# A two-layer backbone kernel: all of v by seven half-size products, partial weight sums by accumulating transfers, the condition stream moved into the heads

## The chip, the cores and the metric

One core of one Trainium2 chip. The metric is device time in microseconds of one execution. Times of before: median 1779.65 us of 3 runs, 1779.38 to 1782.42.

## What is computed

Two layers over 512 latent tokens of width 2048 (and 256 context tokens in the first). The first layer is an even one (mLSTM heads, pooling groups, one output projection), the second an odd one, where the change lies. Of the reference:

```python
sh_l, sc_l, g_l = ada_params(c, ada_w[layer], ada_b[layer])   # silu(c) @ w + b
xm_l = x_lat * (1.0 + sc_l) + sh_l
...
def sgu_mixer(xm, w_in, ln_g, ln_b, w_sp, b_sp):
    u, v, z = jnp.split(xm @ w_in, 3, axis=-1)       # each 2048 wide
    v = layer_norm(v, ln_g, ln_b)
    s = jnp.einsum('hts,bnshc->bnthc', w_sp, vh) + b_sp.T[None, None, :, :, None]
    return u * s.reshape(bsz, seqlen, D_SGU) * jax.nn.silu(z)
...
x_lat = layer_norm(DEEPNORM_ALPHA * x_lat + g_l * (y_l @ w_out_odd[j]), post_ln_g[layer], post_ln_b[layer])
```

## The kernel before, in words

Every float32 operand of a matmul is split in two float32r parts, a rounded one (`hi`, a cast on ScalarE) and the rest (`lo`, a difference on VectorE): `split`, L104 to L106. A product a x b is then three products on TensorE: hi x hi, hi x lo, lo x hi. The program is written in one order; `Flow` (L36) is a planner that counts TensorE time, and lets side tasks (generators that yield how many us to wait) put in their instructions between the products when they are due; `drain` forces the rest of a task out.

**Weights.** The loads of all weights are issued on the SP queue, in program order, 512 KB each. In `ahead` (L159 to L174) a load goes to one of three `wraw` buffers and its two halves are split into `whl` buffers. `newest` holds the newest split's VectorE instruction; a side task that issues under `tc.issue_after(newest[0].ins)` puts its instruction behind that one on VectorE's queue.

**The condition stream.** `ada` (L268 to L292) computes silu(c) @ ada_w on VectorE: 128 steps, each a load of 512 KB into one of three `araw` buffers (SP queue) and one 128x1024 product with an accumulated sum, L280. Its first 96 steps (`ada(range(12), ...)`, L822) are spawned at the first head, one per 2.8 us of planned time. The last 32 steps (`range(12, 16)`, the gate of the second layer) are spawned after the first column block of the first output projection, one per 5.6 us.

**The first output projection.** `out_phase` (L937) with `out0`: column blocks 0 to 2 for all four token blocks, then block 3 for the first 256 tokens, then for the last 256. When a half of the tokens is complete it is normalised, and `finish0` (L1032) transposes it on TensorE, modulates it on ScalarE (L1051, into `mr`) and splits it into `m` (L1052); the first half while the second is multiplied.

**The second layer's input projection.** v (2048 columns): the first 1024 columns are two column blocks by `form_b` (L195), full products of 16 blocks, in the order (0, first half), (0, second half), (1, all), `vseq`; meanwhile `combine` forms the sums of x's quarters (a22 - a21, a11 - (a22 - a21) and so on). The other 1024 columns of v, then z and u in halves, are five jobs of `quarters` (L1131): each takes the 512x2048 by 2048x1024 product as a 2x2 block product with seven half-size products (Winograd's form), numbered 1 to 7. Products 1, 2 and 4 take quarters of x as they are, 3, 5, 6 and 7 take sums. The sums of the weights' quarters are made on VectorE: `t1` = piece 0 + piece 1 (L1169), piece 1 + piece 3 (L1174), `t1` + piece 3 (L1179), piece 2 + `t1` (L1184). A job has 28 steps (7 products x 4 blocks of depth), each of 12 products on TensorE and one split of a 128x1024 unit. Units lie in 7 buffers (4 `whl`, 3 `araw`), raw loads in 4 (3 `wraw`, 1 `crw0`); the split runs `QAHEAD` = 2 steps ahead of the products in program order.

After that come the spatial mixing (`spatial`, a side task on v, which takes the reciprocal deviations from GpSimd, L249), z and u gates, and the second output projection, which is not touched.

Of the kernel before, what the change touches and what calls it, by code (L numbers as in the profile page):

```python
# [16 lines left out]
P = 128  # L17
# [51 lines left out]
def tile_backbone(ctx: ExitStack, tc: tile.TileContext, io: dict, out: bass.AP):  # L69
# [65 lines left out]
    vseq = [(0, H0), (0, H1), (1, ALL)]  # L135
# [3 lines left out]
    for c, _ in vseq:  # L139
        stream += b_raws(io["wv"], c)  # L140
# [3 lines left out]
    raws, parts, used, newest = [], [], [0], [None]  # L144
# [14 lines left out]
    def ahead(p):  # L159
        while len(parts) < min(p + AHEAD + 1, 2 * upto[0]):  # L160
# [107 lines left out]
    def ada(cs, pace):  # L268
        steps = [(f, k) for c in cs for f in range(4 * c, 4 * c + 4) for k in range(2)]
        ts, part = [], None  # L270
        for n, (f, k) in enumerate(steps):
# [6 lines left out]
            if n % 8 == 0:  # L278
                part = cst.tile([P, 4, 2], F32, tag="part", name=nm("part"), bufs=2)
            ve.scalar_tensor_tensor(ts[n], ts[n], 0.5, crow[k], ALU.mult, ALU.mult,  # L280
                                    accum_out=part[:, f % 4, k:k + 1])
# [13 lines left out]
    with ExitStack() as ev:  # L295
# [641 lines left out]
    def out_phase(seq, resid, gate, order, before, norm, finish, hold=0, affine=(), second=None):  # L937
# [15 lines left out]
        def product(c, tbs, before, hold):  # L953
# [3 lines left out]
            def ready(n):  # L957
                if before is not None:
                    before(n)
                if n == KB // 2:  # L960
# [27 lines left out]
        for n, (c, tbs) in enumerate(seq):  # L988
            if n == 1 and second is not None:
                second()  # L990
            for pts in product(c, tbs, before if n == 0 else None, hold if n == len(seq) - 1 else 0):
# [40 lines left out]
    def finish0(hf, z):  # L1032
# [3 lines left out]
        yield 4.0  # L1036
        for k2 in range(8):
# [10 lines left out]
            for j in range(2):  # L1048
                kb = 2 * k2 + j
                m[hf][kb] = big.tile([P, 2, NC], F32R, tag=f"{tag}{kb}", name=nm("xn"))  # L1050
                sc.activation(xt[:, j], pt[:, j * NC:(j + 1) * NC], AF.Identity, bias=B[:, kb:kb + 1], scale=G[:, kb:kb + 1])  # L1051
                split(xt[:, j], m[hf][kb][:, 0, :], m[hf][kb][:, 1, :])  # L1052
# [4 lines left out]
    t_ada2 = []  # L1057
    t_n = out_phase(out0, io["x"], gd[0:1], yorder, y0_ready, norm0, finish0,
                    second=lambda: t_ada2.append(fl.spawn(ada(range(12, 16), lambda n: 5.6))))


    def m_stat(kb, t):
        s = slice((t % 2) * P, (t % 2 + 1) * P)
        return m[t // 2][kb][:, 0, s], m[t // 2][kb][:, 1, s]
# [3 lines left out]

    def v_evac(pts, c):
        for t, pt in pts.items():  # L1070
            s = slice(c * 512, (c + 1) * 512)
            if v[t] is None:
                v[t] = la.tile([P, D], F32, tag=f"z{t}", name=nm("v"))
            sc.copy(v[t][:, s], pt)
            ve.bn_stats(vst[t][:, c, :], v[t][:, s])
# [10 lines left out]
    def combine():  # L1086


        for g in range(4):
            a11, a12, a21, a22 = (mr[i][g + 4 * j] for i in range(2) for j in range(2))  # L1090
            for o, x_, y_, op in ((a22, a22, a21, ALU.subtract), (a21, a11, a21, ALU.subtract),
                                  (a11, a11, a22, ALU.add), (a12, a11, a12, ALU.subtract)):
                with tc.issue_after(newest[0].ins):
                    ve.tensor_tensor(o, x_, y_, op)
                yield PACE
            comb[5, g], comb[7, g], comb[6, g], comb[3, g] = a22, a21, a11, a12
        free = [f"xl{n}" for n in (8, 9, 10, 11, 12, 13, 14, 15, 3, 4, 5, 6, 7, 0, 1, 2)]
        for n in range(8):
            with tc.issue_after(newest[0].ins):
                comb_split((5, 7)[n // 4], n % 4, *((big, tag) for tag in free[2 * n:2 * n + 2]))  # L1100
            yield PACE

    PACE = 2.2
# [5 lines left out]

    def combine2():  # L1110
        for g in range(4):
            comb_split(3, g, (big, f"xh{2 * g}"), (big, f"xh{2 * g + 1}"))
            yield 3.0
        free = [f"mr{n}" for n in (4, 5, 6, 7, 0, 1, 2)] + ["mx"]
        for g in range(4):
            comb_split(6, g, (la, free[2 * g]), (la, free[2 * g + 1]))
            yield 3.0
# [10 lines left out]
    QAHEAD = 2  # L1128
    BUFS = {"wraw": 3, "araw": 3, "whl": 4, "crw0": 1}

    def quarters(jobs):  # L1131


        steps = []
        for n in range(len(jobs)):
            for group in ((1, 5, 7), (2, 3), (6,), (4,)):
                steps += [(n, p_, j) for j in range(4) for p_ in group]
        need = {1: (1, 0), 5: (), 7: (3,), 2: (2,), 3: (3,), 6: (), 4: (2,)}
        loads = [(jobs[n][0], j, piece) for n, p_, j in steps for piece in need[p_]]
        rtags, utags = ["wraw"] * 3 + ["crw0"], ["whl"] * 4 + ["araw"] * 3  # L1140
        n_u = [0]
        raw, made = [], []
        taken = [0]

        def load_to(k):
            while len(raw) < min(k, len(loads)):
                tag = rtags[len(raw) % len(rtags)]
                r = wp.tile([P, 1024], F32, tag=tag, name=nm("qr"), bufs=BUFS[tag])
                q, j, piece = loads[len(raw)]
                dma.dma_start(r, io["wq"][q, j, piece])  # L1150
                raw.append(r)

        def take():
            taken[0] += 1
            load_to(taken[0] + len(rtags) - 1)
            return raw[taken[0] - 1]

        def unit():
            tag = utags[n_u[0] % len(utags)]
            n_u[0] += 1  # L1160
            return wp.tile([P, 1024], F32R, tag=tag, name=nm("wh"), bufs=BUFS[tag])

        t1, b12 = {}, {}

        def prep(n, p_, j):
            if p_ == 1:
                b12[j], x_ = take(), take()
                t1[j] = pair_tile(j)
                ve.tensor_tensor(t1[j], x_, b12[j], ALU.add)  # L1169
            elif p_ == 5:  # L1170
                x_ = t1[j]
            elif p_ == 7:
                x_ = b12[j]
                ve.tensor_tensor(x_, x_, take(), ALU.add)  # L1174
            elif p_ == 2:
                x_ = take()
            elif p_ == 3:
                x_ = take()
                ve.tensor_tensor(t1[j], t1[j], x_, ALU.add)  # L1179
            elif p_ == 6:  # L1180
                x_ = t1[j]
            else:
                x_ = take()
                ve.tensor_tensor(x_, x_, t1[j], ALU.add)  # L1184
            made.append((unit(), unit()))
            newest[0] = split(x_, *made[-1])

        bank = {}
        for i, (n, p_, j) in enumerate(steps):
            while len(made) < min(i + 1 + QAHEAD, len(steps)):  # L1190
                prep(*steps[len(made)])
            at_ = {1: 1, 2: 1, 5: 5, 3: 5, 7: 7, 4: 7, 6: 6}[p_]
            if j == 0 and p_ in (1, 5, 7, 6):
                bank[p_] = [ps() for _ in range(2)]
            pts = bank[at_]
# [309 lines left out]
```

## Time and profile before

| what | value |
|---|---|
| median of 3 runs | 1779.65 us |
| the profiled execution | 1778.18 us |
| its span | 1776.4 us |
| mean granted clock of TensorE | 0.995 |
| TensorE busy | 1735.3 us, 98% of the span |
| VectorE, ScalarE, GpSimd busy | 1215.0, 691.1, 35.0 us |
| moved by DMA | 343.58 MB, mean 193 GB/s |

The span runs from the first to the last instruction of the core; the time of the execution contains it. Busy shares are means over stages with different limits, so each stage is read by itself: the first layer's heads end and its output projection begins at about 894 us, the v stage at 1081, the seven-product stage at 1178, the second output projection at 1588. Windows give busy time and count of records per engine in a stretch, then the granted clock (1.00 is 2.4 GHz) and what the DMA engines did. Matmuls are pipelined: the step from one start to the next is the cost of one, not its duration.

### The profile page before, as it was taken

The numbers are of one execution on the slowest core, as the hardware profiler recorded it, in microseconds if no ns is written. First come the engines' busy times: TensorE is split into PE (matmuls) and PEld (weight loads), VectorE is DVE, ScalarE is ACT, GpSimd is POOL, SyncE is SP. The second block draws the span as 40 slices with busy tenths as digits, with TensorE's granted clock in tenths as the row PEclk, the third lists the DMA queues.
The fourth block names the chain that finished last, engine by engine and source line by source line (L and its number), as shares of the span: only waits on it lengthen the run. The fifth ranks groups of instructions, "written<-read, shape, count | busy, mean of one in ns | idle before, by whom it ended". The sixth has DMA issues, their size and how long they took to land.

```text
span 1776.4 us, 23519 instructions
## 1 busy us (share of the span) xinstructions
PE 1735.3 (98%) x8656; PEld 1419.5 (80%) x8656; DVE 1215.0 (68%) x2140; ACT 691.1 (39%) x1239; POOL 35.0 (2%) x65
## 2 busy tenths in 40 slices
PE   8999999999999999999999999999999999999996
PEld 5677788888788888888887787788888888888884
DVE  4545597778775554564658676767988878875557
ACT  3222332224454355345332247534454444532220
POOL 0000000000000000000000000000000000000004
PEclk9999999999999999999999999999999999999998
DMA  9986298899542332432289656544555454555443
GB/s 370 354 309 232 89 335 312 314 324 358 191 157 84 125 119 87 139 105 73 100 285 327 221 189 215 162 138 158 171 164 180 148 191 137 175 159 167 134 131 106
DMA packets 131130, 343.58 MB, mean 193 GB/s; under 512 B 12622, under 2 KB 22822, under 8 KB 130502
## 3 DMA queue, kind: packets, MB, share of 16 engines
q1 hardware_dynamic: 128710, 335.78, 55.8%
q10 hardware_dynamic: 2304, 6.29, 0.9%
q8 instruction: 68, 1.11, 0.3%
q14 instruction: 48, 0.39, 0.1%
HBM read 319.96 MB, written 22.07 MB: 193 GB/s over the span
## 4 chain that ended last, share of the span: by engine, by line
PE 74%; DMA 13%; DVE 9%; ACT 2%; issue 2%; POOL 0%; SPq 0%; POOLq 0%; DVEq 0%; ACTq 0%
DMA adw<-in_adat_dram 10%; PE ps L1204 7%; PE ps L1203 7%; PE ps L1205 7%; PE ps L187 6%; PE ps L192 6%; PE ps L188 6%; PE ps L204 5%; PE ps L203 5%; PE ps L205 5%; DVE adw L280 3%; PE ps L408 2%; PE ps L410 2%; PE ps L409 2%; PE ps L640 2%
## 5 line engine op out<-in xcount | busy, mean ns | idle before, releaser
L105 ACT CAST wh<-wr 128x512 fp32r<-128x512 f32 x400 | 246.4, 623 | 475.8 <-PE ps L205 173.1
L106 DVE TENSOR_TENSOR wh<-wr,wh 128x512 fp32r<-128x512 f32 x392 | 266.8, 686 | 198.3 <-ACT wh L105 197.0
L187 PE MATMUL ps<-xh,wh 128*128 128x512 f32 x704 | 278.0, 395 | 0.0
L192 PE MATMUL ps<-xh,wh 128*128 128x512 f32 x704 | 275.2, 391 | 0.4 <-DVE wh L106 0.4
L188 PE MATMUL ps<-xl,wh 128*128 128x512 f32 x704 | 275.3, 391 | 0.0
L205 PE MATMUL ps<-wh,yl 128*128 128x512 f32 x512 | 200.2, 391 | 0.0
L204 PE MATMUL ps<-wh,yh 128*128 128x512 f32 x480 | 188.7, 393 | 4.8 <-DVE wh L106 4.8
L203 PE MATMUL ps<-wh,yh 128*128 128x512 f32 x512 | 193.1, 392 | 0.2 <-ACT wh L105 0.2
L280 DVE SCALAR_TENSOR_TENSOR adw<-adw,crow 128x1024 f32<-128x1024 f32 x128 | 156.0, 1220 | 53.7 <-DMA adw<-in_adat_dram 53.0
L192 PEld LDWEIGHTS ps<-xh,wh 128*128 128x128 f32 x704 | 132.2, 188 | 29.2 <-DVE wh L106 0.8
L105 ACT CAST wh<-qr 128x1024 fp32r<-128x1024 f32 x100 | 104.6, 1052 | 128.3 <-PE ps L1205 50.5
L187 PEld LDWEIGHTS ps<-xh,wh 128*128 128x128 f32 x704 | 132.5, 188 | 21.8 <-issue 0.7
L188 PEld LDWEIGHTS ps<-xl,wh 128*128 128x128 f32 x704 | 132.6, 188 | 21.6 <-issue 0.7
L106 DVE TENSOR_TENSOR wh<-qr,wh 128x1024 fp32r<-128x1024 f32 x100 | 121.3, 1218 | 11.5 <-issue 6.4
L1204 PE MATMUL ps<-wh,ch 128*128 128x512 f32 x320 | 126.8, 396 | 0.0
L1205 PE MATMUL ps<-wh,ch 128*128 128x512 f32 x320 | 125.0, 391 | 0.0
L1203 PE MATMUL ps<-wh,ch 128*128 128x512 f32 x320 | 117.6, 396 | 0.0
L203 PEld LDWEIGHTS ps<-wh,yh 128*128 128x128 f32 x512 | 96.4, 189 | 20.9 <-ACT wh L105 1.0
L205 PEld LDWEIGHTS ps<-wh,yl 128*128 128x128 f32 x512 | 96.6, 189 | 19.7
L204 PEld LDWEIGHTS ps<-wh,yh 128*128 128x128 f32 x480 | 90.5, 189 | 26.3 <-DVE wh L106 7.8
L1204 PE MATMUL ps<-wh,xn 128*128 128x512 f32 x240 | 93.7, 390 | 0.0
L1205 PE MATMUL ps<-wh,xn 128*128 128x512 f32 x240 | 93.5, 390 | 0.0
(303 smaller groups left out, 2956.6 us busy)
## 6 DMA issues: line engine op xcount, KB each, us to landing
adw<-in_adat_dram SPq DMA_DIRECT2D x128, 512.0 KB, 5.8
qr<-in_wq_dram SPq DMA_DIRECT2D x120, 512.0 KB, 3.4
wr<-in_wie_dram SPq DMA_DIRECT2D x96, 512.0 KB, 3.6
aw<-in_a_dram SPq DMA_DIRECT2D x64, 512.0 KB, 7.0
wr<-in_woe_dram SPq DMA_DIRECT2D x40, 512.0 KB, 4.9
wr<-in_woo_dram SPq DMA_DIRECT2D x32, 512.0 KB, 3.8
wr<-in_wv_dram SPq DMA_DIRECT2D x24, 512.0 KB, 4.2
w<-in_wie_dram SPq DMA_DIRECT2D x28, 256.0 KB, 4.9
```

The costliest lines, as they stand in the source:

```text
L105: sc.copy(hi, src)
L106: return ve.tensor_tensor(lo, src, f32(hi), ALU.subtract)
L187: te.matmul(pt[:, :n], a, xh_, start=first, stop=False)
L188: te.matmul(pt[:, :n], a, xl_, start=False, stop=False)
L192: te.matmul(pt[:, :n], b, xh_, start=False, stop=last)
L203: te.matmul(pts[t], a, wh, start=n == 0, stop=False)
L204: te.matmul(pts[t], a, wl, start=False, stop=False)
L205: te.matmul(pts[t], b, wh, start=False, stop=n == KB - 1)
L280: ve.scalar_tensor_tensor(ts[n], ts[n], 0.5, crow[k], ALU.mult, ALU.mult, accum_out=part[:, f % 4, k:k + 1])
L1203: te.matmul(pts[t], a, wh[:, s], start=first, stop=False, **more)
L1204: te.matmul(pts[t], a, wl[:, s], start=False, stop=False, **more)
L1205: te.matmul(pts[t], b, wh[:, s], start=False, stop=end, **more)
```

## The change

All of v goes by seven half-size products, as two jobs at the head of the list, six jobs in all. For these two (`first` = 2), products 1 and 2, which need the first 256 tokens only, come first for both jobs, 16 steps; then, per job, 5 and 7 alternating, then 3, 6 and 4. The first unit's split and the first four loads are issued at block 12 of 16 of the projection's last product (`late`). `finish0` of the second half starts 14 us of planned time later than at first 4, in another order, and leaves out the split of the quarter that no product takes as it is. `combine` and `combine2` become one task with a pace of 1.7 us.

A part of the weights' sums is made by transfers that GpSimd issues with `accum_op=ALU.add`, from HBM onto a tile in SBUF. In the two v jobs these are all four sums of a depth block (for product 5: load piece 1 into `t1`, add piece 0; for 7: load piece 1, add piece 3; after product 5's split add piece 3 to `t1`; after product 6's split add piece 2). In the other four jobs `t1` and the sum for product 7 stay on VectorE, and the sums for 6 and 4 are transfers. Loads are issued `LAHEAD` = 3 steps ahead of the splits.

The condition stream's 128 steps are one task in the heads; from step 96 on, one per 5.0 us of planned time, queued on VectorE behind the newest split but one (`older`).

```diff
-    vseq = [(0, H0), (0, H1), (1, ALL)]
-    for c, _ in vseq:
-        stream += b_raws(io["wv"], c)
...
+            older[0] = newest[0]
             newest[0] = split(raws[q // 2][:, (q % 2) * 512:(q % 2 + 1) * 512], hi, lo)
...
+            with tc.issue_after(older[0].ins) if n >= 96 else nullcontext():
+                ve.scalar_tensor_tensor(ts[n], ts[n], 0.5, crow[k], ALU.mult, ALU.mult,
+                                        accum_out=part[:, f % 4, k:k + 1])
...
-                t_ada = fl.spawn(ada(range(12), lambda n: 2.8))
+                t_ada = fl.spawn(ada(range(16), lambda n: 2.8 if n < 96 else 5.0))
...
-            if n == 1 and second is not None:
-                second()
...
-        yield 4.0
-        for k2 in range(8):
+        yield (4.0, 14.0)[hf]
+        for k2 in range(8) if hf == 0 else (0, 4, 1, 5, 2, 6, 3, 7):
...
+                if hf == 0 or k2 > 3:
+                    m[hf][kb] = big.tile([P, 2, NC], F32R, tag=f"{tag}{kb}", name=nm("xn"))
+                    split(xt[:, j], m[hf][kb][:, 0, :], m[hf][kb][:, 1, :])
...
-    PACE = 2.2
+    PACE = 1.7
...
+    QAHEAD, LAHEAD = 2, 3
...
+            self.steps = [(n, p_, j) for p_ in (1, 2) for n in range(first) for j in range(4)]
+            for n in range(len(jobs)):
+                for group in ((5, 7), (3,), (6,), (4,)) if n < first else ((1, 5, 7), (2, 3), (6,), (4,)):
+                    self.steps += [(n, p_, j) for j in range(4) for p_ in group]
+            self.rtags, self.utags = ["crw0"] + ["wraw"] * 3, ["araw"] * 3 + ["whl"] * 4
...
+        def add(self, r, n, j, piece):
+            gp.dma_start(r, io["wq"][self.jobs[n][0], j, piece], accum_op=ALU.add)
...
+        def load(self, n, p_, j):
+            first = n < self.first
+            if p_ == 5 and first:
+                self.t1[j] = pair_tile(j)
+                dma.dma_start(self.t1[j], io["wq"][self.jobs[n][0], j, 1])
+                self.add(self.t1[j], n, j, 0)
+                rs = []
+            elif p_ == 7 and first:
+                rs = [self.raw(n, j, 1)]
+                self.add(rs[0], n, j, 3)
+            elif p_ == 1 and not first:
+                rs = [self.raw(n, j, 1), self.raw(n, j, 0)]
+            else:
+                rs = [self.raw(n, j, {1: 0, 7: 3, 2: 2, 3: 3}[p_])] if p_ in (1, 7, 2, 3) else []
+            self.loaded.append(rs)
...
+        def prep(self, upto):
+            while len(self.made) < min(upto, len(self.steps)):
+                i = len(self.made)
+                n, p_, j = self.steps[i]
+                while len(self.loaded) < min(i + 1 + LAHEAD, len(self.steps)):
+                    self.load(*self.steps[len(self.loaded)])
...
+                self.made.append((self.unit(), self.unit()))
+                newest[0] = split(x_, *self.made[-1])
+
+                if p_ in (5, 6):
+                    self.add(self.t1[j], n, j, 3 if p_ == 5 else 2)
...
+    jobs = [(q, v_sink(q), lambda t, q=q: v_place(q, t, 1)[1]) for q in range(2)]
+    jobs += [(2, z_sink(0), None), (3, u_sink(0), None), (4, z_sink(1), None), (5, u_sink(1), None)]
+    quarters = Quarters(jobs, 2)
+    t_n = out_phase(out0, io["x"], gd[0:1], yorder, y0_ready, norm0, finish0,
+                    late=lambda n: quarters.prep(1) if n == KB - 4 else None)
+    for n, p_ in quarters.run():
+        if (n, p_) == (1, 1):
+            fl.drain(t_n)
+            t_c = fl.spawn(combine())
+        if (n, p_) == (1, 4):
+            t_s[0] = fl.spawn(spatial(0))
```

## Rows read from the trace of the kernel before

**Rows 1.** The page's first part: busy time, share, instructions by engine.

```profile
PE 1735.3 (98%) x8656; PEld 1419.5 (80%) x8656; DVE 1215.0 (68%) x2140; ACT 691.1 (39%) x1239; POOL 35.0 (2%) x65
```

**Rows 2.** Windows: length, busy us (count) of engines, clock, DMA share, GB/s.

```profile
0.00:40.00 40.00, 32.30 (x213) 19.52 (x213) 13.76 (x33) 15.30 (x31) 0.29 (x5) 1.00 0.99 369
280.00:480.00 200.00, 197.54 (x1060) 167.87 (x1058) 154.71 (x345) 67.49 (x152) 0.00 (x0) 1.00 0.85 302
480.00:640.00 160.00, 158.27 (x779) 131.49 (x780) 99.23 (x225) 74.06 (x163) 3.21 (x10) 1.00 0.39 127
1300.00:1560.00 260.00, 260.00 (x1161) 214.44 (x1160) 216.87 (x227) 123.21 (x143) 0.00 (x0) 1.00 0.50 164
```

**Rows 3.** Timeline of TensorE, the v stage: start us, us, what, count.

```profile
1081.41 0.73 PE L203 MATMUL ps<-wh,xn 128*128 128x512 f32 x2
...
1090.16 0.62 PE L203 MATMUL ps<-wh,xn 128*128 128x512 f32 x2
...
1095.60 0.62 PE L203 MATMUL ps<-wh,xn 128*128 128x512 f32 x2
1096.06 2.78 PE L1042 MATMUL ps<-ident,z 128*128 128x128 f32 x24
1098.60 0.48 PE L204 MATMUL ps<-wh,xn 128*128 128x512 f32 x1
...
1177.78 0.39 PE L1203 MATMUL ps<-wh,xn 128*128 128x512 f32 x1
```

**Rows 4.** Windows of the first output projection, one of 2 us last.

```profile
910.00:920.00 10.00, 10.00 (x45) 8.26 (x44) 2.63 (x5) 2.28 (x4) 0.00 (x0) 1.00 1.02 365
...
940.00:950.00 10.00, 8.66 (x38) 6.85 (x37) 9.01 (x16) 1.86 (x3) 0.00 (x0) 1.00 0.90 302
950.00:960.00 10.00, 9.55 (x42) 7.53 (x41) 9.81 (x19) 2.18 (x4) 0.00 (x0) 1.00 0.94 348
960.00:970.00 10.00, 9.58 (x42) 7.94 (x43) 9.38 (x18) 2.17 (x4) 0.00 (x0) 1.00 0.96 317
...
980.00:990.00 10.00, 9.71 (x44) 7.66 (x43) 8.90 (x15) 1.86 (x3) 0.00 (x0) 1.00 0.92 318
990.00:1000.00 10.00, 7.67 (x27) 5.93 (x26) 6.91 (x16) 1.24 (x2) 0.00 (x0) 0.83 0.70 238
...
1020.00:1030.00 10.00, 10.00 (x46) 8.26 (x45) 2.51 (x4) 1.90 (x4) 0.00 (x0) 1.00 0.23 76
...
996.00:998.00 2.00, 2.00 (x6) 1.52 (x6) 1.66 (x3) 0.00 (x0) 0.00 (x0) 0.50 0.94 303
```

**Rows 5.** Waits of ScalarE and SP, 910:1000 us: total, times, longest.

```profile
ACT wh L105 <- DVE adw L280: 19.1, 6, 4.1
ACT wh L105 <- DMA wr<-in_woe_dram: 16.0, 5, 4.1
...
SPq L275 <- DVE adw L280: 42.4, 27, 2.8
```

**Rows 6.** VectorE and ScalarE by group: count, busy us, mean ns, idle before.

```profile
L280 DVE SCALAR_TENSOR_TENSOR adw<-adw,crow 128x1024 f32<-128x1024 f32 x128 | 156.0, 1220 | 53.7 <-DMA adw<-in_adat_dram 53.0
L106 DVE TENSOR_TENSOR wh<-qr,wh 128x1024 fp32r<-128x1024 f32 x100 | 121.3, 1218 | 11.5 <-issue 6.4 <-PE ps L1204 3.6 <-ACT wh L105 0.4
...
L1179 DVE TENSOR_TENSOR pair<-pair,qr 128x1024 f32<-128x1024 f32 x20 | 24.5, 1223 | 15.0 <-DMA qr<-in_wq_dram 15.0
...
L106 DVE TENSOR_TENSOR xn<-xt,xn 128x256 fp32r<-128x256 f32 x32 | 12.4, 419 | 9.8 <-ACT xn L105 9.8
...
L1094 DVE TENSOR_TENSOR xt<-xt,xt 128x512 f32<-128x512 f32 x16 | 10.9, 684 | 0.0
...
L105 ACT CAST wh<-qr 128x1024 fp32r<-128x1024 f32 x100 | 104.6, 1052 | 128.3 <-PE ps L1205 50.5 <-DMA qr<-in_wq_dram 31.2 <-PE ps L1204 20.0
```

**Rows 7.** DMA issues (KB each, us to landing), and GpSimd's largest group.

```profile
qr<-in_wq_dram SPq DMA_DIRECT2D x120, 512.0 KB, 3.4
...
L249 POOL TENSOR_TENSOR rst<-vae,mhalf 128x1 f32<-128x1 f32 (+1 forms) x16 | 14.8, 929 | 906.1 <-DVE vae L247 905.6 <-DVE vm L1279 0.5
```

More of the change, by code (lines that the diff above doesn't have):

```diff
@@ L1 @@
-from contextlib import ExitStack
+from contextlib import ExitStack, nullcontext
 from itertools import chain
@@ L143, in tile_backbone @@
         stream += b_raws(io["woo"], c)
-    raws, parts, used, newest = [], [], [0], [None]
+    raws, parts, used, newest, older = [], [], [0], [None], [None]
     AHEAD, HOLD = 2, 12
@@ L935, in y_stat, with out_phase @@
         return yh[kb][:, t * P:(t + 1) * P], yl[kb][:, t * P:(t + 1) * P]
-    def out_phase(seq, resid, gate, order, before, norm, finish, hold=0, affine=(), second=None):
+    def out_phase(seq, resid, gate, order, before, norm, finish, hold=0, affine=(), late=None):
         z = [la.tile([P, D], F32, tag=f"z{t}", name=nm("z")) for t in range(NT)]
@@ L951, in evacuate, with product @@
                 ve.bn_stats(st[t][:, c, :], z[t][:, s])
-        def product(c, tbs, before, hold):
+        def product(c, tbs, before, hold, late):
             s = slice(c * 512, (c + 1) * 512)
@@ L959, in ready @@
                     before(n)
+                if late is not None:
+                    late(n)
                 if n == KB // 2:
@@ L988, in out_phase @@
         for n, (c, tbs) in enumerate(seq):
-            if n == 1 and second is not None:
-                second()
-            for pts in product(c, tbs, before if n == 0 else None, hold if n == len(seq) - 1 else 0):
+            for pts in product(c, tbs, before if n == 0 else None, *((hold, late) if n == len(seq) - 1 else (0, None))):
                 if c == 3:
@@ L1084, in tile_backbone, with after @@
     comb = {}
     def combine():
+        def after(f, *args):
+            with tc.issue_after(newest[0].ins):
+                f(*args)
+        free = [f"xl{n}" for n in (3, 4, 5, 6, 7, 0, 1, 2)]
         for g in range(4):
             a11, a12, a21, a22 = (mr[i][g + 4 * j] for i in range(2) for j in range(2))
[L1091 to L1094, printed above, removed]
-                yield PACE
@@ L1096, in combine @@
[L1096 to L1100, printed above, removed]
-            yield PACE
-    PACE = 2.2
+            comb[5, g], comb[7, g], comb[6, g], comb[3, g] = a22, a21, a11, a12
+            after(ve.tensor_tensor, a22, a22, a21, ALU.subtract)
@@ new lines, in combine @@
+            yield PACE
+            after(ve.tensor_tensor, a21, a11, a21, ALU.subtract)
+            yield PACE
+            after(comb_split, 5, g, (big, f"xl{8 + 2 * g}"), (big, f"xl{9 + 2 * g}"))
+            yield PACE
+            after(ve.tensor_tensor, a11, a11, a22, ALU.add)
+            yield PACE
+            for i in ((0,), (), (1,), (2, 3))[g]:
+                after(comb_split, 7, i, (big, free[2 * i]), (big, free[2 * i + 1]))
+                yield PACE
+        for g in range(4):
+            after(ve.tensor_tensor, comb[3, g], comb[6, g], comb[3, g], ALU.subtract)
+            yield PACE
+            after(comb_split, 3, g, (big, f"xh{2 * g}"), (big, f"xh{2 * g + 1}"))
+            yield PACE
@@ L1105, in comb_split @@
+        free = [f"mr{n}" for n in (4, 5, 6, 7, 0, 1, 2)] + ["mx"]
+        for g in range(4):
+            after(comb_split, 6, g, (la, free[2 * g]), (la, free[2 * g + 1]))
+            yield PACE
+    PACE = 1.7
     def comb_split(p_, g, *to):
@@ L1108, in comb_split @@
         comb[p_, g] = hi, lo
[L1110 to L1117, printed above, removed]
     def q_stat(p_, j, kk, t):
```

242 lines of the change are left out of this document (99 added, 143 removed).

## The prediction

> **What bounds the kernel now.** I read the busy shares first: TensorE is busy for 98% of the span [rows 1], so what moves the end is the number of products and the places where TensorE waits. Next the windows: over 1300 to 1560 us, inside the seven-product stage, it is busy for 260.00 of 260.00 us, VectorE for 216.87 and the DMA engines for half of the time [rows 2]. In such a stretch an operation taken off VectorE gains nothing by itself. The price of a product comes from TensorE's timeline: 24 products of the v stage take from 1090.16 to 1095.60 us, 0.2267 us each (the duration in a product's row overlaps its neighbours'), and 24 transposes from 1096.06 to 1098.60, 0.106 each [rows 3]. Last, the two stretches in which TensorE loses time, each below with its term.
>
> An execution of 1778.18 us has the span of 1776.4; the median of the runs is 1779.65. The sum is a difference against the profiled execution, and I take it off the median. About 0.2%, 3.6 us, is what a measurement of this kernel can tell from no change.
>
> **Products.** The first half of v is now 2 column blocks x 16 blocks x 4 token blocks x 3 = 384 products; by seven half-size products it is 28 steps x 12 = 336. The 48 that go are 48 x 0.2267 = 10.9 us, all on the path. The 32 transposes of x stay. **-10.9.**
>
> **The condition stream.** The last 32 of 128 vector products leave the first output projection for the heads. Undisturbed, a window of 10 us there holds 45 or 46 product records; the five bad ones hold 38, 42, 42, 44 and 27 [rows 4]. Against 45.5 that is 34.5 products missing, 7.8 us, and it includes the clock: after a wait of 2.33 us the window 996 to 998 shows a granted clock of 0.50, the 1.2 GHz level [rows 4]. The mechanism is in the waits of 910 to 1000 us: the SP queue stands 42.4 us until an adw buffer is free, and the weights' loads queued behind arrive late; ScalarE waits 16.0 us for them and 19.1 us for the adw product itself (its unit shares VectorE's queue) [rows 5]. With the stream gone all of this goes: **-7.8.**
>
> In the heads the same 32 steps bring 32 loads on SP and 32 x 1.22 us on VectorE [rows 6], 39.0 us. From 480 to 640 us VectorE has 99.23 of 160 us busy and would have 138, 86%. The nearest stretch that carries the stream is 280 to 480: VectorE 77% busy, DMA share 0.85, and TensorE idle for 2.46 of 200 us, though 480 to 640 without it also lose 1.73 of 160 [rows 2]. The bounds are 0 and the 7.8 us it cost in the projection; I take **+1.5**, near the head row, because each product is queued behind a split that is already one behind the newest, and comes once per 5 us. Queued behind a late one: the head's weight loads on SP, its attention chain on VectorE.
>
> **The start of v.** From 1081.41 to 1177.78 us [rows 3] are 96.4 us; 384 x 0.2267 = 87.1 and 32 x 0.106 = 3.4 leave 5.9 lost, where ScalarE and VectorE prepare the split of x beside the weights' splits. Afterwards the first 16 steps, 43.5 us, need only the first 256 tokens, and of these only eight column blocks for the first 21.8 us; half of the second half's splits, 8 x 0.42 us on VectorE [rows 6], fall away; and the first weights are loaded and split four blocks before the projection's end. I take **-4**, bounds 0 and -5.9. If what is late next is anything, it is the combining: within steps 8 to 27, 54.4 us, VectorE has 20 weight splits x 1.22, 16 sums and 16 splits of x x 0.69, and about 6 evacuations x 0.69: 50.6 us, 93%. The seven-product stretch runs at 217 of 260, 83%, without a wait [rows 2]. I price this at nothing, with +4 as the other bound: a sum in front of a weight split delays that split, and TensorE waits for it.
>
> **Sums made by transfers.** For jobs 2 to 5 eight sums of 1.22 us [rows 6] per job leave VectorE, 9.8 us; TensorE never waits there, so nothing comes of it. Their eight accumulating transfers per job spread over 76 us of a half-idle DMA; the one tight chain is product 6's split, transfer, product 4's split, four steps or 10.9 us apart, against 3.4 us for a plain load's landing [rows 7]. Price nothing. GpSimd issues 64 of these; its own work here is the four rstd powers of 0.93 us [rows 7], and they now stand behind transfers that wait for splits. Who waits is the spatial task, needed 19 steps later, 52 us: nothing.
>
> The two v jobs are another matter. Their products 5 and 7 come in pairs of steps, 24 x 0.2267 = 5.44 us. Each pair issues two plain loads of 512 KB and three accumulating ones: one before either split, one after product 5's split. On GpSimd's queue the pair after next stands behind that last one, so none can run far ahead. What an accumulating transfer costs, no row shows. A plain one occupies the 16 DMA engines for 1.6 us in the seven-product stretch (524288 B x 0.50 / 164 GB/s) and 1.42 us when they are full (369 GB/s at 0.99) [rows 2]. It cannot be below a plain load: it moves the same bytes from HBM into the same tile. Above, it reads the tile too: two transfers' worth, 2.84 to 3.2 us. I take 1.6, a plain load's row, since half of those reads come from on-chip memory and the full-speed row is one of HBM reads. Then a pair needs 5 x 1.6 = 8.0 us of DMA, 2.56 over. The first pair is loaded during product 2, which needs only one load per 2.72 us; three pairs pay 7.7 us. Against that stands the lead of the splits: seven unit buffers let a split begin when the products three steps back have ended, and the cast of 1.05 and the difference of 1.22 [rows 6] are done 2 x 2.72 - 2.3 = 3.1 us before they are needed. 4.6 us per job, **+9.2** for two. By 1.42 it is 3 x 1.66 - 3.1 = 1.9 per job, 3.8. With a doubled accumulating transfer the pair needs 2 x 1.42 + 3 x 2.84 = 11.36, three pairs pay 17.8, less 3.1 is 14.7 per job, 29 us; by 1.6 and 3.2, 38.
>
> **Sum:** -10.9 - 7.8 - 4 + 1.5 + 9.2 = **-12.0, 1767.7 us.**
>
> **Rivals.** First, *accumulating transfers take twice a plain one* and the kernel is slower. Place: products 5 and 7 of both v jobs, with VectorE and ScalarE waiting on a transfer and the sums of x queued behind. Price 29 to 38 in place of 9.2, so 1779.65 + 8 to + 17: 1788 to 1797. It decides from about 2.3 us per accumulating transfer, where 3 x (3.2 + 3 x 2.27 - 5.44) - 3.1 = 10.6 per job eats the other 21.2 us. For it: the tile must be read back, and the seven-product stretch has idle DMA only on average. Against it: DMA has half its time free, and the full rate in the first 40 us is that of reads from HBM. The Trainium skill, "Collectives: The Full Stack", section "The bandwidth ceiling: the fold count and why AG ≠ RS ≠ AR", speaks for it: adding in a DMA engine is slow for its two source reads on one read ring, not for the add, with a measured ratio of 1.93; by that the estimate is a cost just under double, and no run here shows it.
>
> Second, *the transfers are hidden altogether* (the lead is longer than I count, or they overlap better than busy shares add up) and the start of v loses nothing: -10.9 - 7.8 - 5.9 + 1.5 = -23.1, 1756.6. For it: the plain loads' waits in the seven-product stage cost TensorE nothing today.
>
> Third, *the heads pay the stream back*: its loads stand on the same SP queue in front of head weights, as in the projection. +7.8 in place of +1.5: 1774.0. Against it: 32 products over 160 us instead of some 80, and a DMA share of 0.39 in place of about 0.9 [rows 2, 4].
>
> **Chances.** The forecast 0.40, hidden transfers 0.17, heads 0.10, doubled transfers 0.33, that high because no row has such a transfer. Faster by over 0.2%: 0.36 + 0.17 + 0.09 + 0.02 (doubled, with the start of v all regained and little else lost) = 0.64. Within 0.2%: 0.03 + 0.01 + 0.04 = 0.08. Slower: 0.01 + 0.27 = 0.28. The range reaches from the hidden case to the lower end of the doubled one: 1757 to 1790. The forecast's own, by its bounds (3.8 to 14 for the transfers, 0 to 4 for the rest), is 1759 to 1776.
>
> **What the profile will show.** Right, if the v jobs' products number 672, the projection's 10 us windows hold 45 or 46 throughout with no clock below 1.00, VectorE's sums "pair<-pair,qr" and "qr<-qr,pair" are gone, a few us of TensorE waits stand in the two blocks of products 5 and 7 about 45 and 100 us into v, each ending on a split whose cast waited for a GpSimd transfer, and 480 to 640 us lose at most some 3 us. Wrong, if those blocks show waits at every pair of 5 us and more (doubled transfers), if waits move to the heads, or if VectorE stands at its limit during the combining and the waits there end on VectorE without a transfer behind.

## The result and the profile after

The changed kernel takes 1770.89 us, the median of 4 runs (1769.91 to 1771.86), against 1781.04 for the kernel before in the same timing: ratio 0.9941, 95% interval 0.9924 to 0.9958, so 7.5 to 13.5 us faster. The forecast was 1767.7, 12.0 us below 1779.65. Two later timings beside the experiments give 0.9954 (0.9937 to 0.9971) and 0.9943 (0.9921 to 0.9966): all in all 8 to 10 us.

The profiled execution has a span of 1769.9 us, 6.5 less than the one before. The page first: engines, then DMA queues (packets, MB, share of the 16 engines' span), then DMA issues with KB each and us to landing.

```profile
PE 1725.7 (98%) x8608; PEld 1415.4 (80%) x8608; DVE 1168.8 (66%) x2074; ACT 686.7 (39%) x1209; POOL 93.9 (5%) x129
...
q1 hardware_dynamic: 122182, 323.20, 53.5%
q0 software_dynamic: 9216, 33.56, 10.7%
...
qr<-in_wq_dram SPq DMA_DIRECT2D x112, 512.0 KB, 4.9
...
pair<-in_wq_dram POOLq DMA_DIRECT2D x56, 512.0 KB, 7.1
```

There are 48 products fewer [rows 1]. The new queue q0 carries the 64 accumulating transfers and nothing else: 10.7% of 1769.9 us is 189.4 us of all 16 engines, **2.96 us for each**. On q1, taken over all of its plain transfers, 524288 bytes hold them for 53.5% of 1769.9 us / 323.20 MB x 0.524 MB = 1.54 us. The ratio is 1.92, and I had taken 1.6 us.

In the first output projection the windows of [rows 4] (TensorE's busy us and count, clock, DMA share, GB/s) are now all alike:

```profile
940.00:950.00 10.00, 10.00 (x46) 1.00 0.49 160
950.00:960.00 10.00, 10.00 (x46) 1.00 0.45 143
960.00:970.00 10.00, 10.00 (x46) 1.00 0.34 107
980.00:990.00 10.00, 10.00 (x46) 1.00 0.39 120
990.00:1000.00 10.00, 10.00 (x46) 1.00 0.70 218
```

The SP queue's 42.4 us of waits for an adw buffer [rows 5] are gone, and no wait of TensorE stands between 890 and 1080 us.

In the v stage (TensorE, weight loads, VectorE, ScalarE, GpSimd, then clock, DMA share, GB/s) and in the later jobs:

```profile
1080.00:1120.00 40.00, 40.00 (x195) 33.50 (x194) 33.46 (x49) 29.96 (x51) 4.77 (x5) 1.00 0.87 279
1120.00:1160.00 40.00, 40.00 (x178) 33.09 (x177) 32.81 (x41) 23.34 (x32) 8.74 (x10) 1.00 0.97 238
1160.00:1200.00 40.00, 34.94 (x138) 27.36 (x137) 22.44 (x27) 10.91 (x12) 9.61 (x11) 0.91 1.03 224
1200.00:1240.00 40.00, 40.00 (x177) 33.05 (x176) 26.66 (x26) 18.50 (x19) 4.35 (x5) 1.00 0.76 198
1340.00:1380.00 40.00, 37.32 (x158) 30.39 (x157) 24.74 (x23) 19.78 (x22) 1.73 (x2) 0.96 0.76 228
```

The start of v loses nothing, though the combining falls into these 80 us and VectorE is busy for 66.27 of them. One window stands out: 1160 to 1200 holds 138 products where its neighbours hold 178, with the DMA engines full. 40 products x 0.2267 = **9.1 us**. Another 20, 4.5 us, are missing at 1340 to 1380, and that is not all that the later jobs lose: from their first product (1241.37 us) to the end of the span are 528.5 us, where the kernel before needs 521.8.

What is late at 1160 us is in two timelines, ScalarE's casts and GpSimd's transfer issues (start, us, instruction, idle time before and what ended it):

```profile
1159.39 1.05 ACT L105 CAST wh<-pair 128x1024 fp32r<-128x1024 f32 x1 [1.28 <-PE ps L1212]
1164.93 1.04 ACT L105 CAST wh<-pair 128x1024 fp32r<-128x1024 f32 x1 [4.49 <-DMA pair<-in_wq_dram]
1173.40 1.04 ACT L105 CAST wh<-pair 128x1024 fp32r<-128x1024 f32 x1 [7.42 <-DMA pair<-in_wq_dram]
1176.59 1.04 ACT L105 CAST wh<-pair 128x1024 fp32r<-128x1024 f32 x1 [2.15 <-DMA pair<-in_wq_dram]
1179.09 1.05 ACT L105 CAST wh<-pair 128x1024 fp32r<-128x1024 f32 x1 [1.45 <-DMA pair<-in_wq_dram]
```

```profile
928.03 1.99 POOL L1147 DMA_DIRECT2D pair<-in_wq_dram  x2 [54.72 <-DMA wr<-in_woe_dram]
999.40 0.87 POOL L1147 DMA_DIRECT2D pair<-in_wq_dram  x1 [69.37 <-DMA pair<-in_wq_dram]
1088.19 0.93 POOL L1147 DMA_DIRECT2D pair<-in_wq_dram  x1 [28.43 <-DVE wh L106]
...
1156.96 1.16 POOL L1147 DMA_DIRECT2D pair<-in_wq_dram  x1
1160.32 0.86 POOL L1147 DMA_DIRECT2D qr<-in_wq_dram  x1 [2.20 <-DMA qr<-in_wq_dram]
1162.76 0.86 POOL L1147 DMA_DIRECT2D pair<-in_wq_dram  x1 [1.57 <-issue]
1165.22 0.89 POOL L1147 DMA_DIRECT2D pair<-in_wq_dram  x1 [1.60 <-issue]
1169.53 0.87 POOL L1147 DMA_DIRECT2D pair<-in_wq_dram  x1 [3.42 <-issue]
```

The four issues from 1156.96 on are the sums for product 4 of the first v job. Each is to begin when product 6's split has read the tile. The four issues come 3.2 to 7.4 us after those splits have ended (1153.72, 1156.06, 1160.45 and 1162.18 us); the second job's adds for product 7, the qr line and others like it, stand between them on the same queue. Product 4's casts follow 8.0 to 11.4 us after the issues (1156.96 to 1164.93, 1165.22 to 1176.59). That is the chain from product 6 to product 4, which I had priced at nothing. The lines from 928.03 to 1088.19 are the four first adds of this job's product 5, issued long before the block of products 5 and 7, whose casts begin at about 1116 us. That block, where I had put the loss, pays nothing. The early adds are a part of the reason at most: its other eight adds are issued from 1111.95 to 1136.32 us, inside it.

### The profile page after: what moved, and what is told of

The parts are those of the page before. It is cut to its first block, busy times and chain, and to the rows that moved or that the text cites. A ratio compares the mean times of both kernels' runs of the same rounds, so it can differ in the third digit from the quotient of the medians.

```text
span 1769.9 us, 23424 instructions
## 1 busy us (share of the span) xinstructions
PE 1725.7 (98%) x8608; PEld 1415.4 (80%) x8608; DVE 1168.8 (66%) x2074; ACT 686.7 (39%) x1209; POOL 93.9 (5%) x129
## 3 DMA queue, kind: packets, MB, share of 16 engines
q1 hardware_dynamic: 122182, 323.20, 53.5%
q0 software_dynamic: 9216, 33.56, 10.7%
## 4 chain that ended last, share of the span: by engine, by line
PE 78%; DMA 12%; DVE 7%; issue 2%; ACT 1%; POOL 0%; SPq 0%; POOLq 0%; DVEq 0%; ACTq 0%
DMA adw<-in_adat_dram 7%; PE ps L1211 7%; PE ps L1210 7%; PE ps L1212 7%; PE ps L190 7%; PE ps L185 7%; PE ps L186 7%; PE ps L201 6%; PE ps L203 6%; PE ps L202 6%; DMA qr<-in_wq_dram 2%; DVE adw L280 2%; PE ps L408 2%; PE ps L410 2%; PE ps L409 2%; PE ps L640 2%
## 5 line engine op out<-in xcount | busy, mean ns | idle before, releaser
L105 ACT CAST wh<-wr 128x512 fp32r<-128x512 f32 x352 | 216.4, 621 | 427.9 <-PE ps L203 164.5
L106 DVE TENSOR_TENSOR wh<-wr,wh 128x512 fp32r<-128x512 f32 x344 | 235.0, 687 | 205.0 <-ACT wh L105 199.6
L1211 PE MATMUL ps<-wh,ch 128*128 128x512 f32 x384 | 150.1, 393 | 0.8 <-DVE wh L106 0.7
L1212 PE MATMUL ps<-wh,ch 128*128 128x512 f32 x384 | 149.3, 392 | 0.0
L1210 PE MATMUL ps<-wh,ch 128*128 128x512 f32 x384 | 144.2, 397 | 3.6 <-ACT wh L105 3.6
L105 ACT CAST wh<-qr 128x1024 fp32r<-128x1024 f32 x96 | 100.9, 1057 | 117.4 <-DMA qr<-in_wq_dram 57.3
L106 DVE TENSOR_TENSOR wh<-qr,wh 128x1024 fp32r<-128x1024 f32 x96 | 116.6, 1220 | 33.1 <-ACT wh L105 13.4
L106 DVE TENSOR_TENSOR wh<-pair,wh 128x1024 fp32r<-128x1024 f32 x72 | 87.9, 1221 | 56.7 <-ACT wh L105 18.3
L105 ACT CAST wh<-pair 128x1024 fp32r<-128x1024 f32 x72 | 75.7, 1052 | 107.5 <-PE ps L1212 39.4
L1211 PE MATMUL ps<-wh,xn 128*128 128x512 f32 x288 | 113.9, 396 | 0.7 <-DVE wh L106 0.7
L1212 PE MATMUL ps<-wh,xn 128*128 128x512 f32 x288 | 113.3, 393 | 0.0
L1210 PE MATMUL ps<-wh,xn 128*128 128x512 f32 x288 | 108.0, 399 | 4.3 <-ACT wh L105 4.3
```

The lines of the kernel that those rows point to most:

```text
L105: sc.copy(hi, src)
L106: return ve.tensor_tensor(lo, src, f32(hi), ALU.subtract)
L1210: te.matmul(pts[t], a, wh[:, s], start=first, stop=False, **more)
L1211: te.matmul(pts[t], a, wl[:, s], start=False, stop=False, **more)
L1212: te.matmul(pts[t], b, wh[:, s], start=False, stop=end, **more)
```

## The experiments

Experiments 1 to 3 are timed against the kernel before in one session (before: 1777.55 us), 4 to 6 in a second (1778.84), 7 in a third (1776.99); between sessions only the ratios are compared. The cuts of code are shortened to what an edit comes to: in the kernels of experiments 2, 3 and 5 to 7 the choice stands in a small function, `on_ve`.

**1. The accumulating transfers made plain.** The tile is overwritten: the sums in the weights are left out.

```diff
-            gp.dma_start(r, io["wq"][...], accum_op=ALU.add)
+            gp.dma_start(r, io["wq"][...])
```

> The changed kernel itself, as the base of the runs beside it. All theories: within 0.3% of 1770.9 us. In the profile, if the 4.3 us that the heads ended later in the first trace are chance from one execution to the next, the first output projection begins somewhere between 892 and 900 us; if the moved condition stream costs them, it begins at 898 or later.

> The 64 transfers on GpSimd's queue overwrite their tile in place of adding to it, with the same bytes, queue, waits and order; the weights' sums are left out. Theory 1, an accumulating transfer occupies the DMA engines about twice as long as a plain one (share of the software queue: 10.7% of 1769.9 us over 64 = 2.96 us, against 1.54 us on the hardware queue) and this makes product 4's splits late: the queue's share falls to about 5.5 to 6%, the loss at 1160 to 1180 us nearly goes, and the time falls by 5 to 10 us. Rival, the queue's order and latency (each transfer waits its turn and a split): the share may fall, but the loss at product 4 stays over 5 us and the time falls by less than 3 us.

Measured: the changed kernel again 1769.66 us, ratio 0.9954; with plain transfers 1755.32 (1749.03 to 1757.69), ratio 0.987 (0.985 to 0.989), so 14.3 us less. The page's queue, and two windows of TensorE:

```profile
q0 software_dynamic: 9216, 33.56, 5.7%
```

```profile
1120.00:1160.00 40.00, 40.00 (x178) 1.00 0.76 256
1160.00:1200.00 40.00, 38.52 (x169) 1.00 0.76 264
```

Same bytes, issuer, order and waits: a transfer now holds the engines for 5.7% of 1754.8 / 64 = 1.56 us, and the DMA share falls to 0.76. 9 products are missing in place of 40 (49 in the changed kernel's repetition). It is the accumulating itself that costs: with GpSimd's queue in the same order, most of the loss is gone.

**2. Product 4's sum in the v jobs back on VectorE**, from a plain load.

```diff
+    if p_ == 4 and n < self.first:
+        x_ = rs[0]
+        ve.tensor_tensor(x_, x_, self.t1[j], ALU.add)
-    if p_ in (5, 6):
+    if p_ == 5 or p_ == 6 and n >= self.first:
         self.add(self.t1[j], n, j, 3 if p_ == 5 else 2)
```

> In the two v jobs the sum for product 4 is made by VectorE from a plain load (8 sums of 1.22 us) in place of 8 accumulating transfers. Theory 1, the transfers between products 6 and 4 of the first v job are what TensorE waits for: the 9 us lost at 1160 to 1200 us shrink to 2 or less, 5 to 9 us faster than the changed kernel, 1762 to 1766. Rival, the DMA engines are simply full there (share 1.03) and whichever transfer comes last is waited for: the loss moves to the next job's products 5 and 7, and less than 3 us are gained. Third, VectorE is the limit during the combining: slower by up to 5.

Measured: 1773.67 us (12 runs), ratio 0.9982 (0.9967 to 0.9996): some 4 us slower than the changed kernel. The transfers between products 6 and 4 are gone and the loss is not, by TensorE's windows; the longest wait of ScalarE's timeline follows:

```profile
1120.00:1160.00 40.00, 38.59 (x169) 1.00 0.86 227
1160.00:1200.00 40.00, 35.46 (x148) 0.96 1.00 250
```

```profile
1187.01 1.04 ACT L105 CAST wh<-qr 128x1024 fp32r<-128x1024 f32 x1 [13.01 <-DMA qr<-in_wq_dram]
```

ScalarE now waits 13.01 us for a piece of the second job instead. The engines are as full as before at 1160 to 1200 us (1.00). A late chain alone was the wrong theory: the loss moves on. By TensorE's steps of 12 products (2.72 us when undisturbed), the products up to product 4 of the first job are late by 2.1 us, and by 6.0 in the changed kernel's repetition; the second job's products 5 and 7 by 6.6, and by 5.2 there. Why it ends above the changed kernel rather than beside it is not settled by this run; 9 products are also lost at 1120 to 1160, where the changed kernel loses none.

**3. The later jobs' sums back on VectorE**, for products 6 and 4.

```diff
-    def on_ve(self, n, p_): return False
+    def on_ve(self, n, p_): return n >= self.first
```

(on_ve stands for "this sum is VectorE's" here and below; for product 6 it adds the piece that product 3 has loaded anyway, for product 4 it loads one plainly.)

> In the four later jobs the sums for products 6 and 4 return to VectorE (8 sums of 1.22 us and 4 plain loads per job in place of 8 accumulating transfers). Theory 1: the accumulating transfers there slow the plain loads beside them, and the 4.5 us lost at 1340 to 1380 us go; 3 to 6 us faster than the changed kernel. Rival: that loss is the loads' order (three raw buffers per block, loads three steps ahead), not the transfers; then it stays and the time is within 2 us of the changed kernel's.

Measured: 1767.99 us, ratio 0.9937 (0.992 to 0.9954), not to be told from the changed kernel's 0.9954. That is 1.7 us less than the repetition, not the 3 to 6 of theory 1. The loss at 1320 to 1360 us does go, against the rival, but two others come at 1360 and 1520 us, where the repetition has 175 and 181 products; the first line is the loss in v, which this edit does not touch (TensorE's windows):

```profile
1160.00:1200.00 40.00, 33.51 (x128) 0.91 1.02 227
1320.00:1360.00 40.00, 40.00 (x178) 1.00 0.56 177
1360.00:1400.00 40.00, 38.45 (x163) 0.96 0.41 137
1520.00:1560.00 40.00, 37.57 (x168) 1.00 0.53 165
```

**4. The kernel before with its condition stream ended in the heads**, queued behind `older` as in the change; v and its sums are those of before.

```diff
-    t_ada = fl.spawn(ada(range(12), lambda n: 2.8))
+    t_ada = fl.spawn(ada(range(16), lambda n: 2.8 if n < 96 else 5.0))
...
-    t_n = out_phase(out0, ..., finish0, second=lambda: ...)
+    t_n = out_phase(out0, ..., finish0)
```

> The kernel before with one part of the change alone: the whole condition stream ends in the heads; v, its loads and its sums stay as before. Theory (the first output projection is rid of the 34 to 35 product records it lost, 7.8 us; the heads give back about 3 us, as their end at 895 to 899 us against 894 in the traces after shows): 4 to 5 us below the kernel before, every 10-us window of the projection with 45 or 46 products. Rival (the heads pay all of it back, so that the whole gain of the change comes from the 48 products): within 2 us of the kernel before. Second rival (the heads' end moves only by chance from execution to execution, and the stream is free there): 7 to 8 us below.

Measured: 1775.01 us against 1778.84, ratio 0.9971 (0.9958 to 0.9985): 2.7 to 7.5 us less. The rival by which the heads pay it all back is out; by the medians, 3.8 us, the theory's 4 to 5 is nearly met. The first and last product of the projection, in TensorE's timeline of the kernel before and of this one:

```profile
894.17 0.39 PE L203 MATMUL ps<-wh,yh 128*128 128x512 f32 x1
...
1080.89 0.40 PE L205 MATMUL ps<-wh,yl 128*128 128x512 f32 x1
```

```profile
898.88 0.39 PE L204 MATMUL ps<-wh,yh 128*128 128x512 f32 x1
...
1077.85 0.39 PE L206 MATMUL ps<-wh,yl 128*128 128x512 f32 x1
```

The projection takes 179.0 us in place of 186.7: 7.7, where the forecast had 7.8. The heads end later by 4.7 in this pair. Over the twelve traces that carry the stream in the heads their end lies between 893.9 and 899.6 us, mean 897.2, so they end some 3 us later than in the one trace of the kernel before, with a spread from execution to execution as large. But the moved products do not cost this. The first of them runs at 608 to 614 us. By then the difference is there: TensorE's 3001st matmul starts at 517.0 us in the kernel before and at 521.1 and 521.4 in the changed one and this one, and from it to the projection are 377.2 us before and 377.4 in each of the twelve, one product's time more. Of the moved steps only the first three loads, at 462 to 471 us, come before that. Whether these or chance make the 3 us stays open.

**5. Product 6's sum on VectorE in all six jobs.** Its piece is in SBUF for product 3, so 24 accumulating transfers go and no load comes in.

```diff
+    if p_ == 3:
+        ve.tensor_tensor(self.t1[j], self.t1[j], x_, ALU.add)
-    if p_ in (5, 6):
-        self.add(self.t1[j], n, j, 3 if p_ == 5 else 2)
+    if p_ == 6:
+        self.add(self.t1[j], n, j, 2)
```

> The changed kernel, with the sum for product 6 of all six jobs made by VectorE from the piece that product 3 loads anyway: 24 of the 64 accumulating transfers go and no load comes in. VectorE gets 24 sums of about 1.1 us. Theory (the transfers of the first v job are late since the 16 DMA engines are full at 1160 to 1200 us, above all by accumulating transfers of 2.9 us each, so that taking DMA work away without putting another load in its place helps where moving product 4's sum to VectorE did not): the DMA share of 1160:1200 falls under 1.0, most of the 45 to 49 records lost there come back, and the later jobs' loss at 1320 to 1360 us too: 7 to 12 us below the changed kernel. Rival (VectorE becomes what is late: it is busy 33 of 40 us there, and the sum stands ahead of the split parts in its order): as the changed kernel or slower, with waits on VectorE in place of those on the DMA. Second rival (the first accumulating transfers, those for products 5 and 7, set it alone): within 2 us of the changed kernel, with the loss at the same place.

> The changed kernel again, on the chip of these runs, as their base: 9 to 12 us below the kernel before by the first timing, 8 us below by the second.

Measured: 1764.14 us (1761.22 to 1765.97), ratio 0.9908 (0.9888 to 0.9928); the changed kernel on the same chip 1770.45 (1766.11 to 1774.61). 6.3 us less, and no run of the one reaches the other's: this beats both kernels. The gain is just short of what was expected, and TensorE's windows, after the page's queue, say why:

```profile
q0 software_dynamic: 5760, 20.97, 6.7%
```

```profile
1120.00:1160.00 40.00, 40.00 (x178) 1.00 0.75 192
1160.00:1200.00 40.00, 35.01 (x131) 0.87 0.90 206
...
1320.00:1360.00 40.00, 40.00 (x178) 1.00 0.47 146
```

Here too a transfer holds the engines for 6.7% of 1764.2 / 40 = 2.96 us. The later jobs lose nothing any more, and the whole gain lies there (the table below). At 1160 to 1200 us the loss stays, against the theory, with a share of 0.90: the transfer from product 6 to product 4 is still there, and four casts wait 17.8 us for it and for the second job's pair.

**6. As 5, and the later jobs' sums for product 4 on VectorE too.**

```diff
-    def on_ve(self, n, p_): return p_ == 6
+    def on_ve(self, n, p_): return p_ == 6 or n >= self.first
```

> As the run with all sums for product 6 on VectorE, and in the four later jobs the sum for product 4 too (its piece loaded plainly): 24 accumulating transfers are left, all in the two v jobs. Theory (a transfer costs what it holds of the 16 engines; in the later jobs 1.4 us less for each of 16): 1 to 3 us below the run with product 6 alone. Rival (the later jobs have room, and the sums only move the wait to VectorE): the same or up to 3 us above it.

Measured: 1768.47 us (1766.02 to 1770.76), 4.3 above experiment 5, with no overlap of the runs. The rival has the sign, and the step is over the 3 us that it gave: in the later jobs product 4's sum costs nothing as a transfer and some 4 us as a plain load with a sum on VectorE. Whether VectorE or the load is what is late there, the run does not separate.

**7. As 5, and product 4's sum on VectorE in the first v job; and then every sum of the v jobs; and then every sum.**

```diff
-    def on_ve(self, n, p_): return p_ == 6
+    def on_ve(self, n, p_): return p_ == 6 or n == 0
```

For the other two, products 5 and 7 of a v job are made as in the later jobs (three plain loads, two sums).

> As the run with the sums for product 6 on VectorE, and in the first job of v the sum for product 4 too, from a piece loaded plainly: 36 accumulating transfers are left. Theory (what is still lost at 1160 to 1200 us is the chain from the cast for product 6 over the transfer's issue and its 7 to 10 us to the cast for product 4, and the second job's pair that waits for the same tile): without that chain most of the 47 records lost there come back, 6 to 10 us below the run with product 6 alone. Rival (the engines are full there at 0.90 to 1.04 whatever is moved, as where product 4's sum alone went to VectorE): within 2 us of it, or above, with waits on the plain loads in place of those on the pair.

> As the run with the sums for product 6 on VectorE, and all sums of both jobs of v there, made from three plain loads per k-pair where the changed kernel has two plain and two accumulating ones; 16 accumulating transfers are left, in the later jobs. Theory (the transfers are what is late in v): the DMA share of 1120:1200 falls to some 0.6, the loss at 1160:1200 goes, 9 to 12 us below the run with product 6 alone. Rival (VectorE is the bound there: 33 of 40 us busy in the changed kernel, with some 16 to 24 sums of 1.1 us more, so 37 to 40): the loss stays or moves into 1080:1160, with waits on VectorE's split parts; as the run with product 6 alone or up to 8 us slower.

> The changed kernel without its accumulating transfers: every sum of the weights on VectorE. Theory (that part of the change costs more than it gives): 7 to 14 us below the changed kernel, at or up to 4 us above the run with all of v on VectorE, since the later jobs' sums for product 4 on VectorE cost up to that in the run before. Rival (without them VectorE cannot keep up in v): at the changed kernel or above.

Measured: the first 1761.67 us, ratio 0.9915 (0.9896 to 0.9934), not to be told from experiment 5's 0.9908; the second 1772.42, ratio 0.9975 (0.9961 to 0.9989); the third 1781.17, ratio **1.0027** (1.0012 to 1.0042), slower than the kernel before. The first lost 9 and 28 products in the two windows from 1120 to 1200 us, 37 where experiment 5 lost 47: the 6 to 10 us expected of it did not come. The loss moves as in experiment 2: the steps up to the first job's product 4 are late by 2.2 us instead of 4.6, the second job's products 5 and 7 by 6.4 as against 6.2. VectorE is nearly full before that (its window):

```profile
1120.00:1160.00 40.00, 39.55 (x47) 1.00 0.61 179
```

In the third, the windows of TensorE, that of VectorE, and the waits from 1080 to 1240 us (in all, times, longest):

```profile
1120.00:1160.00 40.00, 30.55 (x114) 0.90 0.60 195
```

```profile
1120.00:1160.00 40.00, 37.07 (x43) 0.90 0.60 195
```

```profile
ACT wh L105 <- DVE pair L1191: 26.2, 7, 7.0
...
PE ps L1216 <- ACT wh L105: 7.4, 8, 2.7
```

The DMA engines have room (0.60), and now ScalarE's casts wait 26.2 us for VectorE's sums, with VectorE busy for 37.07 of 40 us: 64 products are lost in that window. The theory put to the second and the third was wrong; the rival has the sign, and in the second even more than the 8 us it gave. VectorE is the bound of the v stage without the transfers. So the transfers are worth having: with all sums on VectorE the kernel stands 0.0084, about 15 us, above the changed one (1.0027 against 0.9943, each against before on its own chip), although the transfers themselves cost 14.3 us against plain ones. What pays is a mix: product 6's sum to VectorE, where it needs no load, the others left to the transfers.

**All traces in three stretches.** The span of each trace, from TensorE's timeline: to the projection's first product, from there to the first product of the four later jobs (the projection and v), and from there to the end.

| kernel | heads, us | projection and v, us | later jobs to the end, us |
|---|---|---|---|
| before | 894.2 | 360.4 | 521.8 |
| changed | 898.5 | 342.9 | 528.5 |
| changed, beside 1 to 3 | 895.7 | 344.9 | 531.5 |
| changed, beside 4 to 6 | 898.6 | 343.0 | 531.3 |
| 1, transfers made plain | 895.8 | 335.9 | 523.1 |
| 2, product 4 in v on VectorE | 899.6 | 342.7 | 530.4 |
| 3, later products 6 and 4 on VectorE | 896.8 | 345.1 | 528.5 |
| 4, before with the stream in the heads | 898.9 | 352.3 | 525.1 |
| 5, product 6 on VectorE | 898.3 | 344.6 | 521.3 |
| 6, and later product 4 | 895.3 | 343.2 | 527.9 |
| 7, 5 and product 4 of the first job | 897.6 | 342.3 | 521.0 |
| 7, 5 and every sum of v | 893.9 | 355.5 | 520.7 |
| 7, every sum | 897.0 | 356.2 | 527.9 |

The change makes the later jobs 7 to 10 us slower than before, as much as the transfers cost in v. Of what the plain transfers gain over the repetition, 9.0 us lie in v and 8.4 in the later jobs. Experiment 5 gains 10.0 us in the later jobs over the repetition beside it, and nothing in v (1.6 more). In experiment 4 the last stretch, which its edit leaves alone, is 3.3 us longer than in the one trace of before: differences of that size between two traces can be chance.

## Why the prediction was right, and where it was not

The sign and the size came out, 8 to 10 us where 12.0 was forecast. Step by step:

- **Products, -10.9:** as forecast; 8608 stand where 8656 stood.
- **Condition stream out of the projection, -7.8:** shown, 7.7 in the trace of experiment 4, and by the even windows.
- **Stream in the heads, +1.5:** too much for what it names. The heads end about 3 us later (4.3 in the first pair), but the moved products run from 608 to 614 us on, not from 480, and behind 521 us the heads are as long as before, to 0.3 us. What makes the earlier part longer is open.
- **Start of v, -4:** too careful. No product is missing from 1060 to 1160 us, so all 5.9 came back.
- **Combining, 0 with +4 as a bound:** right for the changed kernel, 66.27 of 80 us and no wait. Experiment 7 shows how near the limit lies: at 37 of 40 us TensorE loses.
- **Later jobs, 0:** the first step that failed. "Price nothing" rested on DMA engines that are half idle on average; the stretch from these jobs to the end takes 6.7 us more in the profiled execution and 9.5 to 9.8 in the two repetitions. Some 20 products, 4.5 us, are lost at 1340 to 1380 us, where the DMA share is 0.76, and there product 7's sum on VectorE waits 4.34 us for a piece that is loaded plainly. With plain transfers 8.4 us of it come back, with product 6's sum on VectorE (experiment 5) all of it.
- **Sums by transfers in v, +9.2:** the second. "I take 1.6, a plain load's row" should have been 2.96 us, within the upper bound I named, and the reason given (half of the reads come from on-chip memory) does not hold. The place was wrong too: products 5 and 7 of the first job pay nothing, and the loss stands at its product 4, behind product 6's transfer, to which I had given no price in v at all, and in the later jobs "Price nothing" from a plain load's 3.4 us of landing [rows 7]. It came to 9.1 us in the profiled execution: the right number out of two errors that cancel, so luck. (The 14 us in the forecast's own bounds stand on no working.) In the repetitions it is 9.3 and 11.2 us, of which 2.6 and 5.2 fall on the second job's products 5 and 7. Where the loss shows is not its cause: without the transfer from product 6 to product 4 (experiments 2 and 7) it moves on, and only with plain transfers does most of it go.

The rival of doubled transfers had the rate right and its consequence wrong: its point of 2.3 us was passed, and the kernel did not become slower. Its price of 29 us let each pair of steps pay what the DMA engines lack, less a lead of 3.1 us. But I had said that no transfer can run far ahead on GpSimd's queue, and the timeline shows the first job's first adds for product 5 issued from 928.03 us on, in a projection in which the engines were a third to two thirds idle. That a lead gained there was used up only by 1160 us is my reading; no run took the lead away.

By the three stretches of the two traces: +4.3 in the heads, -17.6 from the projection to the later jobs and +6.7 in the rest, -6.5 by the spans, against -7.9 to -10.1 by the medians. The measured terms -10.9 - 7.7 - 5.9 + 9.1 give -15.4 of the -17.6; where the other 2.2 us come from is open. So the sum of -12.0 came near in part by chance: what the later jobs lose, and it had not priced, the start of v and these 2.2 us in part make good.

The Trainium skill, "Collectives: The Full Stack", section "The bandwidth ceiling: the fold count and why AG ≠ RS ≠ AR", gives 1.93 as the measured ratio of an AllGather's rate to a ReduceScatter's, and lays it to the second source read. For a local load that adds into its tile this trace's ratio is near it, 1.92, and 1.9 against the same transfers made plain; no run here tests the page's reason.

## What to carry to other kernels

Price a sum given to an accumulating transfer at twice a plain load of DMA time, and ask in each stage whether VectorE or the DMA engines have the time. A DMA share of a half on average is no reason to price transfers at nothing: here they cost the later jobs 7 to 10 us. Give the transfers first the sums whose other operand would need a load of its own, and keep on VectorE those whose operand is in SBUF anyway; that paid in the later jobs, while in v the latter changed nothing. Where a transfer waits for one reader of its tile and the next reader for the transfer, look at its landing time under load (8.0 to 11.4 us here), not at that of a quiet queue (3.4 us for a plain load); but removing one such chain gave little back here while the DMA engines stayed full.

## What the runs showed of the hardware

An accumulating transfer of 512 KB from HBM held the 16 engines for 2.96 us in two kernels, against 1.56 us for the same transfer without the addition on the same queue; its median landing was 7.1 us against 4.3, and its issue kept GpSimd for 0.87 us against 0.53. When TensorE had waited 3.15 us for a cast, the 10 us around it ran at a mean granted clock of 0.74, so partly at the 1.2 GHz level, and held 17 products where 45 fit (TensorE's timeline and two of its windows in the changed kernel):

```profile
1174.50 0.55 PE L1210 MATMUL ps<-wh,xn 128*128 128x512 f32 x1 [3.15 <-ACT wh L105]
```

```profile
1160.00:1170.00 10.00, 8.81 (x39) 1.00 1.03 198
1170.00:1180.00 10.00, 6.13 (x17) 0.74 1.03 244
```

Only 3.87 of the 10 us are idle, the time of 17 products; the rest of the 28 missing ones fell to the lower clock.
